# The inverse's running rows: read from DRAM by SyncE instead of copied on GpSimd, in a hybrid decoder step on one core

## The chip, the core and the metric

The kernel runs on one core of a Trainium2 chip. The metric is the device time of one execution in microseconds, the median of several runs. Its engines are TensorE (PE, with its weight loads as PEld), VectorE (DVE), ScalarE (ACT), GpSimd (POOL) and SyncE (SP). SP computes nothing: it issues nearly all DMA transfers, in program order, and stands still at a transfer whose semaphores are not yet there.

## The reference

One trunk layer over 264 tokens (256 of a prompt, 8 single decode tokens), width 2048, all in float32:

```
x = x + 0.5 * swiglu(rmsnorm(x, n1), f1g, f1u, f1d)
proj = rmsnorm(x, nm) @ w_in
o_att  = sliding-window attention with sinks          # 16 heads, prompt and decode
o_rwkv = RWKV-7 time mixing                           # 16 heads of 64, a scan over the tokens:
    sa = einsum('bhij,bhj->bhi', S, -kk_t)
    S  = S * exp(logw_t) + sa (kk_t a_t)^T + v_t k_t^T;   y_t = S r_t
x = x + concat(o_att, o_rwkv) @ w_out
x = x + 0.5 * swiglu(rmsnorm(x, n2), f2g, f2u, f2d)
```

The scan is done by chunks of 64 tokens. Within a chunk the `sa` of later tokens depend on those of earlier ones, and this is solved with the inverse of a triangular matrix of 64 x 64 for each head and chunk: two diagonal blocks of 32 x 32 are inverted element by element, and the block between them is made with matrix products.

## The kernel before

**Products.** Every projection is a `gemm` (line 135) that multiplies 128 x 128 weight blocks with the 264 token columns. Weights come from DRAM in pieces of 128 x 512 (`raw`, six buffers, line 126, issued by SP). ACT casts a piece to `hi` (line 127), DVE, or in part of the products POOL, makes the rest `lo` by a subtraction (line 128, recorded at the helper's line 58). Each of the four blocks in a piece takes three matmuls (line 74): `hi` twice, `lo` once. A `raw` buffer is free again when its `lo` is made; `hi` and `lo` have four buffers each.

**Mixing.** Between the two feed-forward parts, roughly from 768 to 1180 us, the projections for the mixing run, and beside them small tasks as Python generators. `win` (line 394) passes `tick` to `gemm`, and each tick, one for a piece of weights, lets every task advance to its next `yield`. The order that is written this way is then moved about by the framework's scheduler, which works with a timeline of its own; each engine runs its instructions strictly in the resulting order.

**Batches.** Sixteen RWKV heads are handled as eight pairs, two pairs to a batch, so there are four batches (`bat[0]` to `bat[3]`; batch 1 to 4 in the text). `prep` (line 421) makes the masked products `gm` of one pair, and SP writes their diagonal blocks to the DRAM scratch `sa` (lines 509 to 511). When both pairs are done, `chain` (line 548) inverts:

- `X` holds the blocks, 32 of them, each repeated on four groups of 32 partitions. SP reads it with four transfers, one for each group, of 128 KB (line 561). `Y` (named `Xt` in the profile) holds the running rows that become the inverse: group g has rows g, g+4, g+8 and so on. POOL copies them out of `X`, four copies of 32 x 256 (line 562).
- After a pause of `DWAIT` ticks, thirty steps on DVE (lines 567 to 575, two instructions each: `st<-X,Xt` and `Xt<-Xt,st`). The first needs all four groups of both tiles.
- POOL sets the diagonals of `Y` to one (line 578, four memsets, one for each group), SP writes `Y` to the scratch `sb` (line 580) and reads it back in another arrangement as `TT` (line 585). After a second pause DVE transposes (`TN`, line 591), and the matrix products of the chain follow (`zs`, `W`, `PT`, `N`, `Z`, `S`).

`X` and `Xt` have one buffer each, used by all four batches. The third place that the text speaks of is the output projection after the mixing, in three passes over the finished heads; `split` (line 915) casts a finished head on ACT (line 917) first.

Of the kernel before, what the change touches and what calls it, by code (L numbers as in the profile page):

```python
# [30 lines left out]
NWARM = 10  # L31
NGM, NKR, NUV, NTT, NBT = 10, 5, 3, 2, 5
NSTEP = 2
DWAIT = (8, 8, 8, 8)
PW = (2, 1, 3, 2, 2)
ALPHA = math.exp(-0.5)
LKV = 26
# [10 lines left out]
def body(tc, I, O):  # L48
    nc = tc.nc
    V, A, G, TE, SP = nc.vector, nc.scalar, nc.gpsimd, nc.tensor, nc.sync  # L50
# [40 lines left out]
    def pause(n):  # L91
        for _ in range(n):
            yield

    with ExitStack() as ctx:
# [264 lines left out]
        def mixing_body(mx, n2, n3, XD):  # L360
# [3 lines left out]
            def ring(shape, tag, bufs):  # L364
                return mx.tile(list(shape), F32, tag=tag, bufs=bufs, name=uid(tag))
# [23 lines left out]
            scr = [dp.tile([BATCH[b] * 16, 1024], F32, tag=f"sa{b}", name=f"sa{b}") for b in range(nbat)]  # L389
# [148 lines left out]
            def newbatch(i):  # L538
                bt = Batch()
                n = BATCH[i]  # L540
                bt.i, bt.n, bt.left, bt.p0 = i, n, n, sum(BATCH[:i])
                bt.KR, bt.bv = [None] * n, [None] * n
                bt.Gm = [[None, None] for _ in range(n)]
                bt.BT = [None] * n
                bt.UV = ring((P, 4, n, P), "uv", NUV)
                return bt

            def chain(bt):
# [3 lines left out]
                nr = n * 16  # L552
                ng = P // nr
                if ng == 3:
                    ng = 2
                nj = 32 // ng
                X = ring((ng * nr, 32, 32), "X", 1)
                Y = ring((ng * nr, nj, 32), "Xt", 1)
                for g in range(ng):
                    r = slice(g * nr, (g + 1) * nr)  # L560
                    SP.dma_start(X[r], scr[bt.i].rearrange("r (s t) -> r s t", s=32))
                    G.tensor_copy(Y[r], X[r, g:32:ng, :])
                TT = ring((P, n * 4, 64), "TT", NTT)
                for h in range(2):
                    G.memset(TT[h * 64 + 32:h * 64 + 64, :, 0:32], 0.0)
                yield from pause(DWAIT[bt.i])
                for s in range(1, 31):
                    m, w = -(-s // ng), 31 - s
                    t = ring((ng * nr, m, w), "st", 2)
# [12 lines left out]
                for h in range(2):  # L582
                    for blk in range(2):
                        x = h * 64 + blk * 32
                        SP.dma_start(TT[x:x + 32, :, blk * 32:blk * 32 + 32],
                                     scr2[bt.i].rearrange("(h b m) (s t) -> h b s m t", h=2, b=2, s=32)[h, blk])
                yield from pause(DWAIT[bt.i] - 2)
                TN = ring((P, n * 4, 32), "TN", 1)
                for h in range(2):
                    with tc.issue_after(cuts[0]):  # L590
# [9 lines left out]
                for c in range(4):  # L600
                    for k in range(n):
                        for h in range(2):
                            j = k * 4 + c
# [9 lines left out]
                for c in range(4):  # L613
                    for k in range(n):
                        for h in range(2):
                            j = k * 4 + c
# [11 lines left out]
                for k in range(n):  # L628
                    for c in range(4):
                        j = k * 4 + c  # L630
# [11 lines left out]
                for k in range(n):  # L642
                    for c in range(1, 4):
                        x = (k * 3 + c - 1) * 64
                        for h in range(2):
                            r = HALF[h]
                            mm(pP[HALF[1 - h], x:x + 64], W[r, k, c - 1, :], bt.BT[k][r, c, r])
                        for h in range(2):
                            r = HALF[h]
# [7 lines left out]
                for k in range(n):  # L657
                    for c in range(4):
                        x = (k * 4 + c) * 64
                        for h in range(2):  # L660
                            r = HALF[h]
                            mm(pN[r, x:x + 64], bt.BT[k][:, c, r], uv[:, c, k, r])
                for k in range(n):
                    for c in range(4):
                        x = (k * 4 + c) * 64
                        for h in range(2):
                            r = HALF[h]
# [6 lines left out]
                for c in range(1, 4):  # L674
                    ps = mp()
                    for k in reversed(range(n)):
                        for h in range(2):
                            r = HALF[h]
                            mm(ps[r, k * 64:k * 64 + 64], PT[r, k, c - 1, :], S[r, k])
                        for h in range(2):  # L680
                            r = HALF[h]
# [195 lines left out]
            for kind, i in SEQ:  # L877
                if kind == "b":
                    bt = newbatch(i)
                    for k in range(BATCH[i]):  # L880
                        p = bt.p0 + k
                        x = [shifted(2 + 3 * p + j, tmp()) for j in range(3)]
                        spawn(prep(p, bt, k, *x))
                    bat.append(spawn(chain(bt)))
                    bts.append(bt)
                    if len(bat) == len(BATCH):
# [206 lines left out]
```

## Time and profile before

| | us |
|---|---|
| median of 3 runs | 2002.0 (2001.74 to 2003.65) |
| the profiled execution, its own time | 1999.97 |
| span of that execution's trace | 1997.9 |

What lies between the last two rows, 2.07 us, is outside the first and the last instruction. A row of the page's group table gives an engine's line, operation and tiles, the count, the busy time, the mean duration, and the idle time of that engine just before with what ended it. In a timeline row the first number is the start, the second the duration of the row's instructions together, and the bracket the idle time ahead of it with its releaser. For SP a row of several transfers includes its waits between them.

### The profile page before, as it was taken

To read this page: it belongs to the slowest core of one execution; us is meant where nothing else is said; L and a number is where in the kernel's file an instruction comes from. 1 tells how busy PE (TensorE), PEld (TensorE's weight loads), DVE (VectorE), ACT (ScalarE), POOL (GpSimd) and SP (SyncE) were. 2 spreads that over 40 slices of the span, in tenths; PEclk is the share of its full clock that TensorE was granted. 3 is DMA by queue.
4 is the path that set the end of the run, shared out by engine and by line. 5 is a ranking of instruction groups with operands and counts; after the bars stand their busy time and mean duration, and the time that the engine had idled before them with its cause. 6 is when DMAs were issued, how large, how long until landed. Compare 5 with 4: busy or idle time off the path is not lost.

```text
span 1997.9 us, 45891 instructions
## 1 busy us (share of the span) xinstructions
PE 1967.1 (98%) x17212; PEld 1937.1 (97%) x17212; DVE 1305.4 (65%) x2542; ACT 1067.7 (53%) x2127; POOL 344.9 (17%) x453
## 2 busy tenths in 40 slices
PE   9999999999999999999899999999999999999997
PEld 9999999999999999999788899999999999999997
DVE  5865555655556567789677676766666666666655
ACT  5644444444444456776556765654444444444445
POOL 0401001010010122221134553220101001010012
PEclk9999999999999999999899999999999999999999
DMA  7666666655556567554455546565666666666654
GB/s 231 178 192 193 183 193 191 182 184 177 187 177 184 182 196 222 164 158 124 132 156 144 162 143 196 174 182 175 193 186 191 182 191 192 183 191 181 197 177 144
DMA packets 224880, 358.24 MB, mean 179 GB/s; under 512 B 38264, under 2 KB 79888, under 8 KB 224656
## 3 DMA queue, kind: packets, MB, share of 16 engines
q1 hardware_dynamic: 218768, 349.20, 58.4%
q10 hardware_dynamic: 5888, 6.11, 1.0%
q8 instruction: 135, 2.21, 0.5%
q14 instruction: 89, 0.73, 0.1%
HBM read 347.06 MB, written 10.22 MB: 179 GB/s over the span
## 4 chain that ended last, share of the span: by engine, by line
PE 94%; DVE 2%; DMA 2%; ACT 1%; SPq 1%; issue 0%; POOL 0%; DVEq 0%; ACTq 0%; POOLq 0%
PE acc L74 86%; PE m L74 7%; DMA TT<-sb 1%; DVE Xt L58 1%; DVE lo L58 0%; DMA raw<-in_gu 0%; DMA sb<-Xt 0%; DVE st L58 0%; DMA raw<-in_win 0%; ACT t L68 0%; DVE y L58 0%; DMA s<-xsp 0%; ACT hi L127 0%; DVE gm L58 0%; PE m L522 0%
## 5 line engine op out<-in xcount | busy, mean ns | idle before, releaser
L127 ACT CAST hi<-raw 128x512 fp32r<-128x512 f32 (+2 forms) x1304 | 779.0, 601 | 813.3 <-PE acc L74 721.4
L58 DVE TENSOR_TENSOR lo<-raw,hi 128x512 fp32r<-128x512 f32 (+1 forms) x1248 | 857.2, 691 | 540.6 <-ACT hi L127 511.7
L74 PE MATMUL acc<-s,hi 128*128 128x264 f32 x5940 | 1112.5, 287 | 3.0 <-ACT s L917 2.4
L74 PEld LDWEIGHTS acc<-s,hi 128*128 128x128 f32 x5940 | 926.5, 189 | 9.7 <-ACT s L917 2.6
L74 PE MATMUL acc<-s,lo 128*128 128x264 f32 x2970 | 849.4, 287 | 0.0
L74 PEld LDWEIGHTS acc<-s,lo 128*128 128x128 f32 x2970 | 560.6, 189 | 3.0 <-issue 0.7
L74 PE MATMUL acc<-t,hi 128*128 128x264 f32 x2752 | 502.8, 284 | 0.0
L74 PEld LDWEIGHTS acc<-t,hi 128*128 128x128 f32 x2752 | 425.9, 188 | 0.0
L74 PE MATMUL acc<-t,lo 128*128 128x264 f32 x1376 | 388.6, 284 | 0.0
L58 POOL TENSOR_TENSOR t<-t,t 128x264 f32<-128x264 f32 (+1 forms) x148 | 151.1, 1021 | 1149.6 <-ACT hi L127 817.6
L74 PEld LDWEIGHTS acc<-t,lo 128*128 128x128 f32 x1376 | 258.1, 188 | 0.1
L74 PE MATMUL acc<-y,hi 128*128 128x264 f32 x648 | 124.1, 285 | 0.0
L74 PEld LDWEIGHTS acc<-y,hi 128*128 128x128 f32 x648 | 101.0, 188 | 0.2
L74 PE MATMUL acc<-y,lo 128*128 128x264 f32 x324 | 92.0, 284 | 0.0
L58 DVE TENSOR_TENSOR t<-acc,t 128x264 f32<-128x264 f32 x156 | 67.4, 432 | 36.8 <-PE acc L74 36.6
L58 POOL TENSOR_TENSOR lo<-raw,hi 128x512 fp32r<-128x512 f32 x56 | 73.8, 1319 | 65.9 <-ACT hi L127 38.5
L58 POOL TENSOR_TENSOR o<-o,o 128x264 f32<-128x264 f32 x43 | 36.4, 847 | 186.2 <-ACT o L68 182.2
L74 PE MATMUL acc<-o,hi 128*128 128x264 f32 x324 | 63.2, 285 | 0.0
L74 PEld LDWEIGHTS acc<-y,lo 128*128 128x128 f32 x324 | 60.9, 188 | 0.0
L61 DVE SCALAR_TENSOR_TENSOR s<-acc,s 128x264 f32<-128x264 f32 x96 | 40.6, 427 | 16.0 <-PE acc L74 15.5
L74 PEld LDWEIGHTS acc<-o,hi 128*128 128x128 f32 x324 | 50.2, 188 | 0.0
L74 PE MATMUL m<-s,hi 128*128 128x264 f32 x260 | 48.3, 285 | 0.0
(251 smaller groups left out, 1337.8 us busy)
## 6 DMA issues: line engine op xcount, KB each, us to landing
raw<-in_gu SPq DMA_DIRECT2D x688, 256.0 KB, 3.4
raw<-in_dn SPq DMA_DIRECT2D x224, 256.0 KB, 2.9
raw<-in_win SPq DMA_DIRECT2D x152, 256.0 KB, 3.5
raw<-in_dn SPq DMA_DIRECT2D x160, 192.0 KB, 2.7
raw<-in_wout SPq DMA_DIRECT2D x48, 256.0 KB, 3.5
raw<-in_wout SPq DMA_DIRECT2D x32, 128.0 KB, 3.3
s<-xsp SPq DMA_DIRECT2D x16, 132.0 KB, 3.9
ld<-in_sT SPq DMA_DIRECT2D x16, 128.0 KB, 3.5
```

What stands on the lines that cost most here:

```text
L58: return e.tensor_tensor(out=out, in0=a, in1=b, op=op)
L61: return V.scalar_tensor_tensor(out=out, in0=a, scalar=s, in1=b, op0=op0, op1=op1)
L74: TE.matmul(out, lhsT, rhs, start=start, stop=stop, **k)
L127: A.copy(hi[:, :w], raw[:, :w])
```

## The change

`Y` is no longer copied from `X` on POOL. SP reads it from the same scratch `sa` with four more transfers a batch, of 32 KB each, in runs of 32 numbers (128 bytes). The second pause gets its own table `RWAIT`, with the value that `DWAIT[bt.i] - 2` had.

```diff
-DWAIT = (8, 8, 8, 8)
+DWAIT, RWAIT = (8, 8, 8, 8), (6, 6, 6, 6)
...
                 for g in range(ng):
-                    r = slice(g * nr, (g + 1) * nr)
-                    SP.dma_start(X[r], scr[bt.i].rearrange("r (s t) -> r s t", s=32))
-                    G.tensor_copy(Y[r], X[r, g:32:ng, :])
+                    SP.dma_start(X[g * nr:(g + 1) * nr], scr[bt.i].rearrange("r (s t) -> r s t", s=32))
+                    SP.dma_start(Y[g * nr:(g + 1) * nr],
+                                 scr[bt.i].rearrange("r (j g t) -> g r j t", g=ng, t=32)[g])
...
-                yield from pause(DWAIT[bt.i] - 2)
+                yield from pause(RWAIT[bt.i])
```

The scheduler places the new transfers, and moves other instructions with them. Below are pieces of the difference between the two programs' orders; a minus is a row of before alone, a plus a row of the change alone. The first place is batch 3, on SP: `X_13654` and `Xt_13655` are its tiles, `raw_14386` and `raw_14429` two pieces of weights, `TT_12582` belongs to batch 2.

```order
 L585 DMA TT_12582<-sb_10586 32x8x32 x2
-L561 DMA X_13654<-sa_10583 32x1024 x3
+L561 DMA Xt_13655<-sa_10583 32x8x32
+L560 DMA X_13654<-sa_10583 32x1024
+L561 DMA Xt_13655<-sa_10583 32x8x32
+L560 DMA X_13654<-sa_10583 32x1024
+L126 DMA raw_14386<-in_win 128x512
+L561 DMA Xt_13655<-sa_10583 32x8x32
+L126 DMA raw_14429<-in_win 128x512
+L560 DMA X_13654<-sa_10583 32x1024
+L561 DMA Xt_13655<-sa_10583 32x8x32
 L369 DMA ld_14474<-in_sT 128x256
```

The last `X` and the last two `Xt` of this batch now stand behind two pieces of weights, which came after them. The same batch on DVE, where the first step of the inverse (`st_13930`) stands among the work of the next pair:

```order
 L58 TENSOR_TENSOR kr_13807<-t_13167,t_13750 128x256
-L58 TENSOR_TENSOR st_13930<-X_13654,Xt_13655 128x30
 L58 TENSOR_TENSOR pj_10570<-acc_13787,rs 128x264
 L61 SCALAR_TENSOR_TENSOR t_13705<-t_13705,t_13704 128x264
-L58 TENSOR_TENSOR Xt_13655<-Xt_13655,st_13930 128x30
+L58 TENSOR_TENSOR st_13930<-X_13654,Xt_13655 128x30
 L58 TENSOR_TENSOR lo_14206<-raw_14204,hi_14205 128x512
```

The step stands two instructions later, and the subtraction `lo_14206` still right behind. The second place is batch 4, on SP; `X_14737` and `Xt_14738` are its tiles:

```order
 L126 DMA raw_15492<-in_win 128x512
+L561 DMA Xt_14738<-sa_10584 32x8x32
+L560 DMA X_14737<-sa_10584 32x1024
+L126 DMA raw_15557<-in_win 128x512
+L561 DMA Xt_14738<-sa_10584 32x8x32
+L821 DMA bk_15518<-vnd 32x2x128 x2
```

Here the last `Xt` stands behind `raw_15557`. On POOL, in the same batch, where POOL makes the `lo` of some pieces:

```order
-L562 COPY Xt_14738<-X_14737 32x256
 L829 COPY bk_15518<-o_14971 64x8 x2
-L562 COPY Xt_14738<-X_14737 32x256
 L578 MEMSET Xt_14738 32x8
-L562 COPY Xt_14738<-X_14737 32x256
 L58 TENSOR_TENSOR lo_15250<-raw_15248,hi_15249 128x512
-L562 COPY Xt_14738<-X_14737 32x256
 L58 TENSOR_TENSOR lo_15367<-raw_15365,hi_15366 128x512
```

The copies are gone; the memset of the first group's diagonal stays ahead of `lo_15250`. The third place is ACT at the start of the output projection, where `s_16487` is the cast of the first finished head:

```order
 L68 ACTIVATE stc_15769<-sta_15767,vec 128x2
+L917 CAST s_16487<-y_12906 128x264
 L68 ACTIVATE bk_15795,stb_15800<-bk_15795,sta_15799 128x129 x2
 L68 ACTIVATE stc_15801<-sta_15799,vec 128x2
 L800 COPY o_15447<-m_15853 128x256
-L917 CAST s_16487<-y_12906 128x264
```

The cast has moved ahead of the decode attention's exponentials and one copy.

## The prediction

> **What bounds the kernel now.** I began with the page's head and its engine table, to see whether one engine fills the span.
>
> ```profile
> span 1997.9 us, 45891 instructions
> PE 1967.1 (98%) x17212; PEld 1937.1 (97%) x17212; DVE 1305.4 (65%) x2542; ACT 1067.7 (53%) x2127; POOL 344.9 (17%) x453
> ```
>
> TensorE is busy 1967.1 of 1997.9 us. A change on SP and POOL can move the time only through the 30.8 us in which TensorE is idle, or by adding to them. Where these lie I asked of the view by stages (columns: stretch, length, then busy time and count of PE, PEld, DVE, ACT, POOL, then granted clock, DMA share, GB/s).
>
> ```profile
> 16.00:768.00 752.00, 752.00 (x6183) 751.82 (x6184) 460.08 (x778) 374.33 (x680) 97.56 (x97) 1.00 0.62 188
> 900.00:920.00 20.00, 18.85 (x388) 16.43 (x387) 18.22 (x64) 12.17 (x35) 3.48 (x9) 0.91 0.43 124
> 960.00:980.00 20.00, 16.89 (x297) 15.45 (x295) 16.52 (x49) 12.91 (x35) 6.08 (x18) 0.91 0.63 170
> 980.00:1000.00 20.00, 15.57 (x200) 13.82 (x193) 12.14 (x48) 9.29 (x23) 0.23 (x2) 0.83 0.26 72
> 1040.00:1060.00 20.00, 17.00 (x287) 15.04 (x287) 18.54 (x65) 9.22 (x19) 7.53 (x9) 0.86 0.47 141
> 1100.00:1120.00 20.00, 17.61 (x145) 15.17 (x146) 13.45 (x47) 14.02 (x47) 12.58 (x24) 1.00 0.74 238
> ```
>
> The feed-forward stretch has no idle TensorE at all. The mixing has, in single stretches in which DVE is nearly full (18.54 of 20 us at 1040), and there the clock is granted only in part. The view of waits names who ended each idle time of TensorE (us in total, times, longest).
>
> ```profile
> PE m L522 <- DVE t L58: 3.7, 1, 3.7
> PE m L74 <- DVE N L58: 3.6, 1, 3.6
> PE m L74 <- DVE TN L591: 3.1, 2, 1.7
> PE m L74 <- DVE st L58: 3.0, 1, 3.0
> PE acc L74 <- ACT s L917: 2.4, 1, 2.4
> ```
>
> So TensorE waits five times for 2.4 us or more in all, four of them on DVE, which runs in order and holds the inverse's steps between the subtractions and everything else. **A DVE that stands still in the mixing delays TensorE if no slack follows; SP matters through what DVE and the weights wait for.**
>
> **The change, part by part.** Sixteen POOL copies go and sixteen SP transfers come. The nearest rows are the tiles' own: `X` and its copies, and `TT`, which like the new transfers is 32 KB in runs of 32 numbers.
>
> ```profile
> L561 SPq DMA_DIRECT2D X<-sa x16: 303/417/548, 839.5 to 1034.7; - x16
> L562 POOL COPY Xt<-X x16: 386/396/751, 842.2 to 1041.0; 32x256 f32<-32x256 f32 x16
> DMA to landing us min/median/max: 2.4/3.5/5.3
> L585 SPq DMA_DIRECT2D TT<-sb x16: 310/438/451, 893.4 to 1075.3; - x16
> DMA to landing us min/median/max: 2.0/3.6/4.1
> ```
>
> I price a new transfer by `TT`: 0.44 us of SP's time, 3.6 us to landing, between 2.0 and 4.1. Removed are 16 x 0.396 = 6.3 us of POOL, which is busy 17% and on no row of TensorE's waits.
>
> *SP's time.* Four more issues are 1.8 us a batch, 7.0 us in all. They push the weights behind them, but SP does not lack time and the weights are not late:
>
> ```profile
> SPq L126 <- DVE lo L58: 912.2, 921, 6.2
> ACT hi L127 <- PE acc L74: 33.8, 44, 2.6
> ```
>
> SP stands 912 us waiting for a `raw` buffer to come free, and in the mixing what ACT's casts wait for is TensorE's release of the `hi` buffers, not a landing. I take 0; with that cover gone it would be the 7.0 us.
>
> *Batch 1.* The order puts the last `Xt` 2.2 us behind the place of the last `X` before (five more issues of 0.44).
>
> ```profile
> 841.21 0.43 SPq L561 DMA_DIRECT2D X<-sa  x1
> 849.36 0.18 DVE L58 TENSOR_TENSOR st<-X,Xt 128x30 f32<-128x30 f32 x1
> ```
>
> 841.2 + 2.2 + 4.1 = 847.5 at the latest by `TT`, and DVE's first step is at 849.4: 0.
>
> *Batch 2.* The last `Xt` now follows the first of five pieces of weights, which waits for its buffer until 899.11.
>
> ```profile
> 899.11 6.79 SPq L126 DMA_DIRECT2D raw<-in_win  x5
> 901.94 0.18 DVE L58 TENSOR_TENSOR st<-X,Xt 128x30 f32<-128x30 f32 x1
> 902.04 0.68 DVE L58 TENSOR_TENSOR lo<-raw,hi 128x512 fp32r<-128x512 f32 x1
> ```
>
> It is issued at about 899.5 and lands at 903.1 (901.5 to 903.6). In the new order one subtraction precedes the step, so DVE reaches it at 901.94 + 0.6 = 902.5 and stands 0.6 us (0 to 1.1). The stage has DVE at 18.22 of 20, so I count all of it: **+0.6**.
>
> *Batch 3.* The last `X` and two `Xt` stand behind two pieces of weights, whose buffers are freed by two subtractions that DVE reaches only after its transposes.
>
> ```profile
> 964.75 1.13 SPq L126 DMA_DIRECT2D raw<-in_win  x2
> DMA to landing us min/median/max: 3.5/3.5/3.6
> 964.04 1.49 DVE L58 TENSOR_TENSOR lo<-raw,hi 128x512 fp32r<-128x512 f32 x2
> 967.78 0.17 DVE L58 TENSOR_TENSOR st<-X,Xt 128x30 f32<-128x30 f32 x1
> 968.22 0.41 DVE L61 SCALAR_TENSOR_TENSOR t<-t,t 128x264 f32<-128x264 f32 x1
> 987.21 0.37 PE L74 MATMUL m<-N,PT 64*64 64x64 f32 x2 [3.59 <-DVE N L58]
> ```
>
> (The second row is these two pieces' own time to landing.) SP is free of them at 965.9, then come the last `X` and the last `Xt`, which is issued at 966.4. By the pieces just ahead it lands at 969.9 (968.4 to 970.5 by `TT`). DVE reaches the step two instructions later than before, at 968.5, and stands 1.4 us (0 to 2.0). From there DVE goes without a pause to `N`, for which TensorE already waits 3.59 us: nothing takes it up. With the wait come the late `lo`, which TensorE wants only later. I take **+1.5**.
>
> *Batch 4.* Here POOL makes some of the `lo`, and two effects meet.
>
> ```profile
> 1033.31 0.88 SPq L561 DMA_DIRECT2D X<-sa  x2
> 1041.01 0.33 SPq L126 DMA_DIRECT2D raw<-in_win  x1
> 1035.37 0.62 ACT L127 CAST hi<-raw 128x512 fp32r<-128x512 f32 x1 [0.89 <-PE acc L74]
> 1038.63 0.39 POOL L562 COPY Xt<-X 32x256 f32<-32x256 f32 x1 [2.78 <-DMA X<-sa]
> 1039.69 1.29 POOL L58 TENSOR_TENSOR lo<-raw,hi 128x512 fp32r<-128x512 f32 x1
> 1039.94 1.59 DVE L58 TENSOR_TENSOR lo<-raw,hi 128x512 fp32r<-128x512 f32 x1 [4.72 <-ACT hi L127]
> 1041.82 0.19 DVE L58 TENSOR_TENSOR st<-X,Xt 128x30 f32<-128x30 f32 x1 [0.29 <-POOL Xt L562]
> ```
>
> The `raw` at 1041.01 waits for the `lo` that ends at 1040.98 on POOL. That `lo` had its cast since 1036.0 and stood behind a copy that waited 2.78 us for `X`. In the new order only the memset of the first group is ahead of it, which waits for the first `Xt`. That transfer goes out where the second `X` did, at 1033.3, and lands between 1035.7 and 1038.6 (the limits of `X`, since the queue is full of weights here); I take 1037.2. The `lo` ends 1.3 later, at 1038.6; the `raw` follows at once, the last `Xt` at 1039.0, landing 3.5 later at 1042.5. Before, DVE took the step at 1041.8: **+0.7**. At best DVE is there when its own `lo` is done in the 0.68 of the row above instead of 1.59, at 1040.6, which gains 1.2; at worst both transfers take 5.3 and the `Xt` lands at 1045.7, which costs 3.9. In the new order the `kr` products, which give back the PSUM buffers that TensorE waits for here, and `N` come one pair of steps sooner, 2 x 0.23 by the pace of these steps: **-0.5**.
>
> *The output projection.* TensorE's wait of 2.4 us ends with a cast on ACT that now stands earlier.
>
> ```profile
> 1104.81 0.39 ACT L68 ACTIVATE bk<-bk,sta 128x129 f32<-128x129 f32 x1
> 1106.02 0.41 ACT L917 CAST s<-y 128x264 fp32r<-128x264 f32 x1
> ```
>
> It moves ahead by 1106.02 - 1104.81 = 1.2 us. DVE and POOL still have to make the rest of that head, so I take **-1.0** (0 to -1.2).
>
> *POOL beside DVE.* In batch 3 the two subtractions at 964.04 took 1.49 us with copies running beside them; at 0.6 from one to the next and 0.69 for the last they would take 1.29. One such meeting in a batch or two: **-0.3** (0 to -0.8).
>
> Sum: 0 + 0.6 + 1.5 + 0.7 - 0.5 - 1.0 - 0.3 = **+1.0** on 1999.97, which is 2001.0. The runs shown have their median 2.0 above that execution, so I forecast **2003.0**, between 1999.5 and 2006.5 if not all ends fall together. That is no change: about 0.2%, 4 us, is what a measurement of this kernel can tell from none.
>
> **The rivals.**
>
> *Slower, through the last `Xt` of each batch.* The place is SP: the transfer stands behind a weight piece that waits for a buffer, and DVE, in order, stands at the first step with subtractions behind it. It decides when the `Xt` of batch 4 lands after 1044, that is when it takes the 5.3 us that `X` took there at most: 1039.0 + 5.3 = 1044.3, a stall of 2.5. With batch 2 and 3 at their ends, 1.1 + 2.0 + 2.5 - 0.5 = +5.1, and the cast's gain lost to the same lateness: 2007. For it speaks that this stretch has the longest landings; against it, that 32 KB is a quarter of what `X` moves.
>
> *Slower, through late weights.* SP's 7.0 us become TensorE's, because the `raw` pieces behind the transfers land after ACT wants them: 2009. Against it stand the 912 us.
>
> *Faster, because DVE is freed.* POOL's copies and DVE's steps meet at the memory, and a `lo` is no longer stuck behind a landing. What the rows allow: the 1.2 of batch 4 at its best, its 0.5, the cast's 1.2, no stall in batches 2 and 3, and of the 6.3 us of copies the half that lies in batches 3 and 4, where TensorE waits on DVE, 3.1. Together -6.0: 1996. The 1.49 row shows only 0.2 for three copies, which speaks against it. The Trainium skill's page "Advanced Engine Details and Errata", section VectorE Performance Modes, says that GpSimd shares VectorE's second port, so that the two can block each other. By that rule taken whole, the gain would be up to all of the copies' time; the trace agrees in kind, with the 0.2 us, and not in size.
>
> That the change does nothing but swap is not among them: the second pause is 6 ticks as before, in all four batches, so no tick moves.
>
> **How the numbers follow.** No change (2003.0) 0.38, slower by the last `Xt` 0.30, slower by late weights 0.12, faster 0.20. Of the first, 0.02 lies above 2006. So faster 0.20, same 0.36, slower 0.44. The range for 8 in 10 goes from 1996 to 2009: it takes in the second case and the likelier halves of the two at the ends.
>
> **What would show it.** In the new trace, DVE's `st<-X,Xt` of 128x30 should be idle before for `DMA Xt<-sa` in batches 2, 3 and 4, by about 0.6, 1.5 and under 1 us, and not in batch 1. TensorE's wait for `N` should be 5 instead of 3.6 us, that for `ACT s` 1.4 instead of 2.4. The `lo` on POOL in batch 4 should start before 1039, measured from the same landmarks. I am wrong if ACT's casts wait for landings of `raw`, if a TensorE wait of over 2 us stands at a place where there was none, or if the steps of the inverse never wait.

## The result, and the profile after

The change took 2005.40 us (median of 12 runs, 2004.04 to 2008.96) beside 2001.35 for the kernel before (12 runs, 1997.97 to 2005.61): ratio 1.0021, 95% interval [1.0012, 1.0030], so slower by 4.05 us. The forecast was 2003.0 with a range of 1996 to 2009. The range holds the time. But the forecast's sum was +1.0, which it called no change, and the runs say +4, with an interval that leaves out no difference. The profiled execution took 2004.15 us. In its page's head and engine table,

```profile
span 2002.4 us, 45887 instructions
...
PE 1967.0 (98%) x17212; PEld 1937.1 (97%) x17212; DVE 1302.9 (65%) x2542; ACT 1070.3 (53%) x2129; POOL 338.4 (17%) x437
```

TensorE does the same work in the same 1967 us, and is idle 35.4 us instead of 30.8. POOL lost 6.5 us of work. The view of what ended TensorE's idle time (total, times, longest) tells where the 4.6 us are:

```profile
PE m L74 <- DVE N L58: 4.6, 2, 4.0
PE m L522 <- DVE t L58: 3.3, 1, 3.3
PE m L74 <- DVE TN L591: 3.0, 2, 2.0
PE acc L74 <- ACT s L917: 2.2, 1, 2.2
PE m L74 <- DVE st L58: 2.1, 1, 2.1
PE m L74 <- DVE t L791: 1.9, 2, 1.5
PE m L74 <- POOL shc L407: 1.8, 1, 1.8
PE m L74 <- DVE gm L58: 1.5, 2, 1.1
PE m L74 <- ACT XD L491: 1.2, 1, 1.2
```

Of the five large waits of before, four became shorter, by 1.6 together, and `N` grew by 1.0, of which a second, short wait is 0.6. What is new are small ones at other places: the copy `t` of line 791 (1.9), `shc` (0.5 before), `gm` (0.8 before) and `XD`. None is a wait for a landing.

The first steps of the inverse, which the prediction watched, stand so in VectorE's timeline (batches 2, 3, 4; the bracket is the idle time ahead):

```profile
904.10 0.19 DVE L58 TENSOR_TENSOR st<-X,Xt 128x30 f32<-128x30 f32 x1 [1.32 <-DMA raw<-in_win]
...
972.93 0.19 DVE L58 TENSOR_TENSOR st<-X,Xt 128x30 f32<-128x30 f32 x1 [3.17 <-DMA Xt<-sa]
...
1046.12 0.19 DVE L58 TENSOR_TENSOR st<-X,Xt 128x30 f32<-128x30 f32 x1 [3.19 <-DMA Xt<-sa]
```

VectorE stands 1.3, 3.2 and 3.2 us, where stalls of 0.6, 1.4 and under 1 us were forecast. (In batch 2 the last `Xt`, issued at 900.07, landed at 903.81, just ahead of the step.) In batch 3 SP's own timeline shows why:

```profile
966.18 0.35 SPq L126 DMA_DIRECT2D raw<-in_win  x1
966.58 1.29 SPq L561 DMA_DIRECT2D Xt<-sa  x1
967.98 0.55 SPq L126 DMA_DIRECT2D raw<-in_win  x1
968.57 0.43 SPq L560 DMA_DIRECT2D X<-sa  x1
969.04 0.55 SPq L561 DMA_DIRECT2D Xt<-sa  x1
```

An `Xt` between the two pieces takes 1.29 us of SP and the last one 0.55, where the price from `TT` was 0.44. The group of all sixteen:

```profile
L561 SPq DMA_DIRECT2D Xt<-sa x16: 542/566/1295, 840.0 to 1042.6; - x16
...
DMA to landing us min/median/max: 2.9/3.6/4.1
```

The landing (3.6 us, 4.1 at most) was priced right; the issue was not.

### The profile page after: what moved, and what is told of

Read it like the earlier page. It is cut to its first block, busy times and chain, and to the rows that moved or that the text cites. A ratio compares the mean times of both kernels' runs of the same rounds, so it can differ in the third digit from the quotient of the medians.

```text
span 2002.4 us, 45887 instructions
## 1 busy us (share of the span) xinstructions
PE 1967.0 (98%) x17212; PEld 1937.1 (97%) x17212; DVE 1302.9 (65%) x2542; ACT 1070.3 (53%) x2129; POOL 338.4 (17%) x437
## 4 chain that ended last, share of the span: by engine, by line
PE 92%; DVE 4%; DMA 2%; ACT 1%; issue 1%; SPq 1%; POOL 0%; DVEq 0%; ACTq 0%; POOLq 0%
PE acc L74 85%; PE m L74 6%; DVE lo L58 1%; DVE st L58 1%; DVE Xt L58 1%; DMA raw<-in_gu 0%; DMA TT<-sb 0%; DMA Xt<-sa 0%; ACT L68 0%; DMA s<-xsp 0%; ACT t L68 0%; DMA xg<-in_xT 0%; ACT hi L127 0%; DVE t L61 0%; DVE y L58 0%
```

## The experiments

Each run's difference is its median less that of the kernel before in the same set (11 runs of it, 5 of the two fastest, 10 of the repeat; 26 to 33 of before).

| run | what is changed | us | ratio [95%] |
|---|---|---|---|
| after2 | the change again | +4.5 | 1.0022 [1.0013, 1.0031] |
| h12 | row transfers in batches 1, 2 only | -0.3 | 0.9997 [0.9988, 1.0006] |
| h34 | in batches 3, 4 only | +2.7 | 1.0009 [1.0001, 1.0018] |
| h3 | in batch 3 only | +0.5 | 1.0001 [0.9992, 1.0010] |
| h4 | in batch 4 only | +4.2 | 1.0017 [1.0009, 1.0026] |
| dummy | copies kept, transfers to nowhere | +4.2 | 1.0021 [1.0012, 1.0029] |
| one | one transfer a batch, ahead of `X` | +4.6 | 1.0023 [1.0015, 1.0032] |
| gq | row transfers on GpSimd's queue | +3.9 | 1.0019 [1.0010, 1.0028] |
| bdw_9 | before, pauses 8, 9, 9, 9 | -2.3 | 0.9989 [0.9980, 0.9997] |
| dw_9 | the change, pauses 8, 9, 9, 9 | -7.6 | 0.9965 [0.9953, 0.9978] |
| dw_899 | the change, pauses 8, 8, 9, 9 | +2.5 | 1.0016 [1.0007, 1.0025] |
| dw_10 | the change, pauses 8, 9, 10, 10 | -9.6 | 0.9952 [0.9938, 0.9966] |

Theory A came first: VectorE's stalls at the inverse's first step are the cost. Its rivals were B, the other order of the instructions around them and where TensorE's clock is lowered, and C, each added transfer costs by itself. D, one place of B's order, was added after the first two sets.

**Which batches (h12, h34).** In both, the copy of line 562 is back where the condition doesn't hold; h34 has `(2, 3)`.

```diff
+                    if bt.i in (0, 1):
+                        SP.dma_start(Y[r], scr[bt.i].rearrange("r (j g t) -> g r j t", g=ng, t=32)[g])
+                    else:
+                        G.tensor_copy(Y[r], X[r, g:32:ng, :])
```

> SyncE reads the running rows in batches 1 and 2 alone; in 3 and 4 GpSimd copies them as before. Theory A (VectorE stands at the inverse's first step for the last block or row transfer, and TensorE pays it in batches 3 and 4): the stall of 1.3 us in batch 2 is back, those of 3.2 us in batches 3 and 4 are gone; time 0 to +1.5 us on before, ratio 1.000 to 1.0008. Theory B (the stalls don't matter; the other order of the instructions around them, and where the half-clock pieces fall, make the 4 us): the time goes anywhere between -2 and +4 us whatever the stalls do. Theory C (each of the added transfers costs by its issue and its load on the queues): half of the whole change, +2 us.

> SyncE reads the running rows in batches 3 and 4 alone; in 1 and 2 GpSimd copies them as before. Theory A: VectorE stands about 3.2 us at the first step of batches 3 and 4 and not in batch 2; time +2.5 to +4 us, ratio 1.0012 to 1.002, nearly all of the change. Theory B: between -2 and +4 us, not tied to the stalls. Theory C: half of the change, +2 us.

h12 came out at -0.3 us although its stall in batch 2 was 1.7 us and TensorE's wait for `shc` 1.8 as in the change: neither leaves anything in the time that the runs can tell. h34 has +2.7, which its interval ([1.0001, 1.0018], some 0.2 to 3.6 us) doesn't tell from C's +2; it is h12 that speaks against C, which wanted half in each. So the larger part of the cost sits in batches 3 and 4, as A said.

**Transfers that nothing waits for (dummy).** The kernel before, with four more transfers a batch into a tile `Q` that nothing reads (five of the eight rows of each group, so five eighths of the bytes):

```diff
                     G.tensor_copy(Y[r], X[r, g:32:ng, :])
+                    SP.dma_start(Q[r], scr[bt.i].rearrange("r (j g t) -> g r j t", g=ng, t=32)[g][:, 0:5])
```

> The kernel before with its copies on GpSimd, and beside them four more transfers a batch on SyncE behind each block transfer, of 32 x 5 x 32 into a tile that nothing reads. Theory A: these are waited for by nothing; what they cost is the block transfers that stand behind weights by their doing. Where the last block transfer keeps its place ahead of the pieces of weights, no stall; +0 to +2 us. Theory B: between -2 and +4 us. Theory C: they take the same issues as the change, so the time is that of the change, +4 us, though nothing waits for them.

+4.2 us: C's number, and twice A's upper end. VectorE's waits for the first steps are here, in the view of its waits, only

```profile
DVE st L58 <- POOL Xt L563: 2.2, 2, 1.3
```

where the change has 7.7. The stall shrinks to less than a third and leaves the time where it was, so it isn't what sets the time here. Either C was right, or something else that dummy shares with the change.

**One larger transfer (one).**

```diff
+                SP.dma_start(Y, scr[bt.i].rearrange("r (j g t) -> g r j t", g=ng, t=32))
                 for g in range(ng):
                     SP.dma_start(X[g * nr:(g + 1) * nr], scr[bt.i].rearrange("r (s t) -> r s t", s=32))
-                    SP.dma_start(Y[g * nr:(g + 1) * nr],
-                                 scr[bt.i].rearrange("r (j g t) -> g r j t", g=ng, t=32)[g])
```

> The running rows of a batch are read with one transfer of 128 x 8 x 32, issued ahead of the four block transfers, in place of four. The last transfer that VectorE needs is then a block one that stands behind one piece of weights less than in the change, about where it stood before. Theory A: no stall of more than 0.5 us at the first step in batches 3 and 4; time within 1 us of before, ratio 0.9995 to 1.0005. Theory B: still +2 to +4 us if the half-clock pieces fall as in the change, else anything. Theory C: a quarter of the issues, +1 us.

+4.6 us, a miss for A and for C; B had allowed anything. The groups of its transfers on SP, the row one first:

```profile
L559 SPq DMA_DIRECT2D Xt<-sa x4: 567/580/683, 840.9 to 1035.2; - x4
...
L561 SPq DMA_DIRECT2D X<-sa x16: 368/422/2945, 841.6 to 1040.2; - x16
...
DMA to landing us min/median/max: 3.4/4.0/6.6
```

The large transfer itself is issued in 0.58 us, but the transfer right behind it takes 2.2 to 2.95 us of SP in every batch, and landings of the block transfers reach 6.6 us. In batch 4 VectorE stands 7.1 us, the longest of all these traces (the releaser named landed with the last block transfer, issued at 1040.2):

```profile
1046.83 0.19 DVE L58 TENSOR_TENSOR st<-X,Xt 128x30 f32<-128x30 f32 x1 [7.09 <-DMA s<-xsp]
```

**The other queue (gq).**

```diff
-                    SP.dma_start(Y[g * nr:(g + 1) * nr],
+                    G.dma_start(Y[g * nr:(g + 1) * nr],
```

> The sixteen row transfers go out on GpSimd's queue instead of SyncE's, so that SyncE's order is that of before again and nothing stands in front of the last block transfer that did not before. Theory A (the stall at the inverse's first step in batches 3 and 4, made by transfers that stand behind weights in SyncE's queue, is the cost): the stall is gone or under 1 us unless GpSimd issues late; time within 1.5 us of before, ratio 0.999 to 1.0008. Theory C (sixteen more transfers of 256 runs of 128 bytes cost by themselves, wherever they are issued): +4 us, ratio 1.002.

+3.9 us, against A. GpSimd spends 0.58 us on each issue and they land after 4.5 us (median), later than on SP (3.6):

```profile
L561 POOL DMA_DIRECT2D Xt<-sa x16: 584/584/802, 841.1 to 1036.9; - x16
...
DMA to landing us min/median/max: 2.4/4.5/5.6
```

The stall isn't gone either: VectorE now stands for the block transfers, which SP issues and which land after 4.3 us (median) here and 3.5 before.

```profile
DVE st L58 <- DMA X<-sa: 6.5, 2, 6.2
```

The Trainium skill's page "DMA: Bandwidth & Descriptors", section Issuing engines are not separate DMA queues, says that transfers started by ScalarE, SyncE or GpSimd run on the same 16 DMA engines and interleave there. These landings agree.

**A longer pause (dw_9, and bdw_9 as its control).**

```diff
-DWAIT, RWAIT = (8, 8, 8, 8), (6, 6, 6, 6)
+DWAIT, RWAIT = (8, 9, 9, 9), (6, 6, 6, 6)
```

> The change with the pause ahead of the first step one tick longer in batches 2 to 4, so that VectorE comes to the step when the transfers have landed; the sixteen transfers are all there. Theory A: the stall shrinks from 3.2 us to under 1 us in both batches, and the time falls by 2 to 4 us against the change, to within 2 us of before, less what the later inverse itself costs, which the next run shows by itself. Theory C: it stays at the change's +4 us or above.

> The kernel before with the same longer pause in batches 2 to 4 and no new transfer: what a later inverse costs by itself. Theory A: within 2 us of before, and the run with the transfers and the longer pause lies within 1.5 us of this one. Theory C: that run lies 4 us above this one.

With all sixteen transfers in it, dw_9 is 7.6 us faster than before and 5.35 below its control (1998.57 - 1993.22). C wanted 4 us above the control and is refuted, with h12 beside it: no cost of the transfers as such shows. But A, which wanted the two within 1.5 us, falls by the same run. It forecast a stall of under 1 us, and in dw_9 the timeline of VectorE has, in batch 3,

```profile
969.06 0.19 DVE L58 TENSOR_TENSOR st<-X,Xt 128x30 f32<-128x30 f32 x1 [7.03 <-DMA Xt<-sa]
```

twice the stall of the change, in a kernel 12 us faster. How long VectorE stands at this step doesn't tell the time by itself. What counts, as I read it, is which work TensorE asks for behind it.

**The change again (after2).**

> The change once more, unaltered, on the chip of these runs, with a second profile. All theories: ratio 1.0015 to 1.0027. Theory A: the stalls at the first step of batches 3 and 4 recur, 3.2 us each within 0.5. Theory B (half-clock pieces that fall elsewhere make the difference): the pieces or the stalls stand elsewhere in this profile.

+4.5 us. The stall of batch 3 recurs (3.2), that of batch 4 is 2.4 where A wanted 3.2 within 0.5, and a new one of 1.5 stands in batch 1. The clock doesn't make the difference between the change and before: the mean of the granted clocks of the runs is 0.9912 for the change (12 runs) and 0.9913 for before (33 runs). B's clock part is out for the mean of the runs; single profiles are another matter (below).

**One batch alone (h3, h4).** The same edit as h12, with `bt.i == 2` and `bt.i == 3`.

> SyncE reads the running rows in batch 3 alone, GpSimd copies them in the others. The orders of batches 1, 2 and 4 and of the output projection are those of before. Theory A, as it now stands (the 3.2 us stall of batch 3 is paid by TensorE, that of batch 4 isn't): VectorE stands about 3 us at batch 3's first step, TensorE's idle time between 960 and 1000 us grows by 1.5 to 2.5 us, the half-clock pieces may follow; time +1.5 to +3 us, ratio 1.0005 to 1.0015. Theory D (the cost lies in the last reciprocals and copies before the output projection's end, which stand in another order in the change): 0 to +0.5 us, no TensorE wait at 1170 us.

> SyncE reads the running rows in batch 4 alone. The orders of batches 1 to 3 are those of before, that of the last heads' work at 1160 us is the change's. Theory A as it now stands: VectorE stands about 3 us at batch 4's first step and TensorE pays nothing there, its wait near 1055 us no longer than 3.0 us. Theory D: TensorE's wait of 1.5 us near 1170 us for the copy t is there, and the time is +1 to +2 us, ratio 1.0004 to 1.001. If the two together make the change, this run and the one before add up to +3 to +4 us.

Batch 3 alone costs nothing that the runs can tell (+0.5), with a stall of 3.7 us, as D said and against A. Batch 4 alone costs what the whole change costs, +4.2; D had only +1 to +2 for it, so D's size was missed. (h34, with both, has +2.7; the intervals of h34 and h4 overlap.) Where, a table shows that I worked out from the traces: all have 17212 TensorE instructions, so it compares the starts of the ones with the same number, in us later than in the trace of before (where the order differs a little, it is right to a few tenths).

| place in the trace of before | after | h3 | h4 |
|---|---|---|---|
| 960 (ahead of batch 3's steps) | +1.5 | 0.0 | +0.2 |
| 980 | +3.8 | +4.1 | +0.1 |
| 1050 (batch 4's steps) | +3.5 | +3.0 | -0.8 |
| 1060 | +0.6 | -1.4 | -0.1 |
| 1100 | +0.8 | -1.5 | +0.8 |
| 1160 | +2.5 | 0.0 | +2.5 |
| 1180 | +4.0 | 0.0 | +4.1 |
| 1985 (the end) | +5.0 | 0.0 | +5.0 |

In h3 batch 3's stall makes TensorE 4 us late, and at 1060 all of it is gone. In the view of its waits the 3.0 us that before has for `DVE st` near 1053 have shrunk to this:

```profile
PE m L74 <- DVE st L58: 0.6, 1, 0.6
```

TensorE came late to a place where it had stood and waited anyway. That is 2.4 of the 4.4 us between 1050 and 1060; the other 2.0 go with the clock, which over 1040 to 1070 is 0.89 before and 1.00 in h3. In h4, where nothing precedes, that wait grew, where A had it no longer than 3.0:

```profile
PE m L74 <- DVE st L58: 4.1, 1, 4.1
...
PE m L74 <- DVE t L794: 1.9, 2, 1.5
```

From 1160 on h4 and the change run alike, and this is D. TensorE's timeline of before, then of the change, at the products of the last decode attention:

```profile
1169.45 0.40 PE L74 MATMUL acc<-s,hi 128*128 128x264 f32 x2
1169.78 0.86 PE L74 MATMUL m<-t,s 128*64 128x256 f32 x6
1170.57 0.39 PE L74 MATMUL acc<-s,lo 128*128 128x264 f32 x1
```

```profile
1169.15 0.86 PE L74 MATMUL m<-t,s 128*64 128x256 f32 x6
1171.51 0.43 PE L74 MATMUL m<-t,s 128*64 128x128 f32 x2 [1.49 <-DVE t L791]
1171.87 0.39 PE L74 MATMUL acc<-s,lo 128*128 128x264 f32 x1
```

In the change these products stand earlier among the output projection's. The copy `t` that they need stands on VectorE some instructions behind a reciprocal that has moved back by five places, and which itself waits for ACT:

```profile
1165.45 1.80 DVE L723 RECIPROCAL t<-t 128x264 f32<-128x264 f32 x1 [0.71 <-ACT t L68]
...
1171.17 0.28 DVE L791 COPY t<-m 128x128 f32<-128x128 f32 x1
```

This wait of 1.5 us is in the change (both its traces), h34, h4 and dummy, and in none of before, h12, h3 and one. So is a second thing: the feed-forward behind it. In the view by stages over the same 700 us (PE's count in the first bracket), before, then the change:

```profile
1250.00:1950.00 700.00, 700.00 (x5749) 699.23 (x5748) 451.23 (x775) 337.99 (x598) 78.91 (x81) 1.00 0.62 185
```

```profile
1250.00:1950.00 700.00, 700.00 (x5741) 699.24 (x5741) 451.13 (x775) 337.89 (x597) 78.89 (x81) 1.00 0.62 185
```

TensorE is never idle and at full clock in both, and does 8 instructions less: 8 x 700/5749 = 1.0 us. The count is 5749 in h3, h12 and one too, and 5741 in after2, h4, h34 and dummy: the same two groups (the programs with other orders have counts of their own, 5735 to 5755). Together 2.5 us, in each of these programs that has the new order near 1160 us and in none that has the old one, whether VectorE stood at batch 4's step for 3.8 us (h4) or 1.3 (dummy).

But D isn't the only way to +4. `one` and gq have no wait for `t` there and cost 4.6 and 3.9. By the measure of the table, `one` is 4.5 us late at 1040, 7.9 at 1050 and 6.3 from 1100 to the end: here a stall at batch 4's step does stay in the time. Its granted clock is lower too, 0.9901 in the mean of its runs beside 0.9913 before. The trace of gq (one of its slower executions, 2007.33 us) is 5.6 late at 1160 already, and its feed-forward is as slow as the change's, 5740 instructions.

**More pauses (dw_899, dw_10).** `DWAIT` is (8, 8, 9, 9) and (8, 9, 10, 10).

> The change with pauses of 8, 8, 9 and 9 ticks: batch 2 as in the change, batches 3 and 4 a tick later. If the gain of 8, 9, 9, 9 lies in batch 3 and 4's own first steps, most of it is here, ratio 0.997 to 0.999. If it lies in batch 2, whose rows then stand behind batch 3's transfers and whose products come later, the stalls and the time stay near the change's, ratio 1.000 to 1.002.

> The change with pauses of 8, 9, 10 and 10 ticks ahead of the first step. The gain of the longer pause came from work of the inverse that no longer stands ahead of the products TensorE waits for, at the price of a later inverse. If more of it helps still, the ratio is under 0.9965; if the later end of batches 3 and 4 now shows in TensorE's waits for the last heads, it is 0.997 to 1.001.

The gain needs batch 2's longer pause (dw_899 is +2.5; no run has that pause alone), and dw_10 has it with still longer pauses in batches 3 and 4 (its interval overlaps dw_9's): 1991.49 us beside 2001.13, the fastest kernel here, 0.9952 [0.9938, 0.9966]. Its waits of TensorE begin

```profile
PE m L74 <- DVE TN L591: 4.0, 1, 4.0
PE m L74 <- DVE st L58: 2.9, 1, 2.9
PE m L74 <- POOL shc L407: 1.6, 1, 1.6
```

The 3.7 for `t` and 2.4 for `ACT s` are gone, and `N` is down from 3.6 to 0.7. On VectorE the wait for the landing of `TT`, which no part of the prediction had looked at, fell between before (first row) and dw_10 (second):

```profile
DVE TN L591 <- DMA TT<-sb: 13.7, 4, 6.4
```

```profile
DVE TN L591 <- DMA TT<-sb: 2.2, 1, 2.2
```

Part of these gains goes with the clock. Its mean over the runs is 0.9936 in dw_9 and 0.9944 in dw_10, beside 0.9913 before: over some 2000 us at most 4.6 and 6.2 us, an estimate that holds only where TensorE has work. In the control bdw_9 it is 0.9934, so the clock doesn't tell dw_9 from its control. Why the row transfers gain more from the pause than the copies do no run separates.

## Why the prediction was right in its range and wrong in its reasons

The measured time lies in the range. But "slower" (chance 0.44) is what happened, not the "no change" of the forecast (+1.0), and it came another way than the rivals had it.

**SP's time, 0: right.** The 7.0 us of issues (more like 9, at 0.566) show no cost as such: dw_9 has them all and is 5.35 us below its control. Late weights fell as a rival: ACT's casts wait less for `raw` than before (the weights of the feed-forward 7.5 us in all instead of 8.8, those of the output projection 0.6 instead of 1.6), and in the mixing not at all.

**The output projection, -1.0: the step that failed.** The forecast saw the cast `s` move ahead by 1.2 us and booked it. The wait went from 2.4 to 2.2, because ACT had meanwhile waited 1.4 us for VectorE's `sta` in front of it, as its timeline in the change has it:

```profile
1105.42 0.51 ACT L68 ACTIVATE t<-t,sta 128x256 f32<-128x256 f32 x1 [1.41 <-DVE sta L65]
...
1107.01 0.40 ACT L917 CAST s<-y 128x264 fp32r<-128x264 f32 x1
```

The same reshuffle set the products `m<-t,s` and their copy against each other, +1.5, and the feed-forward ran 1.0 slower: -1.0 was to be about +2.3 (-0.2 + 1.5 + 1.0). This alone takes the sum from +1.0 to +4.3, where the runs have +4.05; that they agree so well is luck, as the next points show: several terms are off and cancel. The order of all engines behind the change was there to be read; only ACT's was used there.

**Batch 2, +0.6; batch 3, +1.5: stalls too small, and their price too large.** Measured against TensorE's own lateness at the place (the table's +1.5 at 960, and +0.3 ahead of batch 2), the steps were late by 1.9 us (904.10 - 901.94 - 0.3) and 3.7 (972.93 - 967.78 - 1.5). The forecast's landings made it 1.2 and 2.1. In batch 3 the order ahead of the prediction has one `Xt` between the two pieces of weights, and only the last `X` and the last `Xt` behind both; the forecast had SP free of both at 965.9 and so left out that one's issue, 0.44 by its own price and 1.29 in the run. But h12 and h3 price the two batches at -0.3 and +0.5. "Nothing takes it up" was wrong: TensorE is late at `N` (the wait is 4.0, towards the 5 forecast), and in h3 the wait near 1053 takes up 2.4 of it. In the change that wait is only 0.9 shorter, and about 2 us there are the clock's.

**Batch 4, +0.7 - 0.5: the landing right, the rest not.** Less the 3.5 us by which everything was late there, the step stands at 1042.6; the forecast said 1042.5. So the rival of a late last `Xt`, which wanted a landing after 1044, did not come true by its own condition, near as its 2007 is to the measured time. The `lo` on POOL starts at 1040.1, which less 3.5 is 1036.6 and before 1039, as forecast. The stall is 3.2 and not 0.7 since VectorE came earlier, as the case "at best" had it: in h4, its `lo` ahead of the step takes 0.69 instead of 1.59. The -0.5 did not come; TensorE's wait there is 0.9 shorter in the change and 1.1 longer in h4.

**POOL beside DVE, -0.3, and the rival "faster".** DVE's busy time fell from 1305.4 to 1302.9, 2.5 us for 6.3 us of copies, more than the 0.2 us seen at one place. The Trainium skill's page "Advanced Engine Details and Errata", section VectorE Performance Modes, has the two engines share a port, and this may be that. But bdw_9, with all sixteen copies, has 1303.1, so the 2.5 us aren't shown to be the copies' doing; what of them reached TensorE is open.

**"No tick moves": right, and the wrong thing to look at.** With one or two ticks more the same change gains 7.6 and 9.6 us, and the copies gain 2.3 (bdw_9).

**What stays open.** Of the +4.05, the new order behind 1160 us accounts for some 2.5 in five traces. The rest isn't settled: the waits near 1053 and the lowered clock differ from profile to profile. No run has the new order at 1160 without four more transfers of SP in batch 4, so D is seen by its presence in five traces and its absence in four, and wasn't taken away alone; and one of these four, `one`, is as slow without it. That D makes the 2.5 us is argued from the places in the traces, not shown by a run that differs in D alone.

## What to carry to other kernels

Where a scheduler sets the order, a small edit is priced by two lists: what it does at its own place, and what its reshuffle does to every engine until the orders meet again. Read the second list for each engine that TensorE waits for, not for one. A stall of an engine counts only as far as no later wait of the bottleneck takes it up, and a pause that was tuned for one way of fetching data has to be tuned again for another before the way is judged.

## What the runs showed of the hardware

- A row transfer of 32 x 8 x 32 (runs of 128 bytes) takes 0.54 us of SP at least, the block transfers of four times the bytes 0.42, and `Q` with 32 x 5 x 32 also 0.42. Behind one transfer of 128 x 8 x 32, itself 0.58, the next issue takes 2.2 to 2.95 us.
- TensorE's clock falls after some waits and not after others of the same length. Over 1100 to 1120 us, before has a wait of 2.4 us and a clock of 1.00; the change has one of 2.2 and a clock of 0.91 (h3 and h12 have 2.4 and 0.91):

```profile
1100.00:1120.00 20.00, 17.62 (x152) 14.96 (x146) 12.76 (x50) 11.71 (x39) 10.13 (x17) 0.91 0.71 222
```

  20 x 0.09 = 1.8 us of clock are gone there. Over 1040 to 1070 it is the other way, 0.89 before and 1.00 in the change:

```profile
1040.00:1070.00 30.00, 27.00 (x387) 24.62 (x387) 27.08 (x98) 16.95 (x42) 13.27 (x19) 0.89 0.42 125
```

```profile
1040.00:1070.00 30.00, 27.44 (x410) 25.20 (x409) 23.25 (x89) 16.40 (x41) 11.42 (x12) 1.00 0.54 150
```

  That is 30 x 0.11 = 3.3 us at most between two profiles, and part of why the table of TensorE's places passes +0.6. There the clock goes with TensorE's wait near 1053 us: 0.83 with 4.1 us in h4, 0.89 with 3.0 before, 1.00 with 2.1 in the change and with 0.6 in h3. The Trainium skill's page "TensorE: Matmul & The Clock Gate", section Part 1: The HAM clock gate (the "warmup" mystery), says that the window in which activity is watched runs free, so that the transition depends on where in it the work falls. The rows agree with that. It also has the clock fall after an idle window of some 3.4 us; here a wait of 2.2 us was enough, and the measurement decides.
- The same feed-forward, with no idle TensorE and full clock, runs at 5749 or 5741 instructions in 700 us (5735 to 5755 over all programs), and the order of VectorE's, ACT's, POOL's and SP's work in it is the same in before, the change, h3 and h4. What differs is the work that ended before it; how that carries over is not known.
